# Empty places of the experts skipped by a bound on the index in the row gathers and scatters, with four fixed buffers for gathered rows

## The chip, the cores and the metric

The kernel runs on one core of one Trainium2 chip. The metric is device time in microseconds (us); lower is better. A core has five engines with instruction queues of their own, each worked off in order: PE (TensorE, matrix products), DVE (VectorE), ACT (ScalarE), POOL (GpSimd) and SP (SyncE, which here only starts transfers). Transfers run on 16 DMA engines that all queues share. "Landing" of a transfer is the moment its completion reaches the waiting engine.

## The reference, cut to what matters

A first block (two layers of a mixer) and a second block (linear attention, retention) come before the part that changes: a mixture of experts over 1024 tokens, with 32 experts, two for each token.

```python
def hier_moe(h, w_rg, b_rg, w_re, b_re, w_gate, w_up, w_down):
    ...
    expert_id = g_sel[:, None] * EXPERTS_PER_GROUP + top_i.astype(jnp.int32)
    ...
    def expert_block(args):
        xb, e = args
        hid = jax.nn.silu(xb @ w_gate[e]) * (xb @ w_up[e])
        return hid @ w_down[e]

    y = lax.map(expert_block, (x_pad.reshape(NB, MOE_BLOCK, D), block_e)).reshape(P, D)
    out = jnp.zeros((T, D), jnp.float32).at[tok_pad].add(y.astype(jnp.float32) * w_pad[:, None])
```

Each token of 1024 numbers goes to two experts, so 2048 pairs of token and expert are worked on. How many fall to each expert depends on the inputs. With the inputs of this case the counts, from the largest, are 173, 149, 149, 148, 145, 137, 136, 124, 98, 89, 70, 64, 62, 57, 57, 55, 49, 44, 44, 43, 28, 23, 20, 19, 18, 17, 10, 6, 6, 5, 3 and 0.

## The kernel before

The experts are the last large stage, after the output projection of the second block (`po`, which adds into `x`). The router (`router`, `choose`, `ranks`, `places`) finds for each token its two experts and its rank there, sorts the experts by their counts, and makes two index tables: `idh` (which token stands at a place, for reading) and `idy` (which row of the result, for writing). Each expert in the sorted order has a fixed number of places, whatever its count: ten have 192 (two blocks, of 128 and 64), four 128, four 96, eight 64 and six 48 (`CAPS`); that is 42 blocks with 3616 places for 2048 pairs. A place beyond an expert's count is empty; `index` adds 2048 + p to its index, so that it points behind the real rows:

```python
    hrow = dr.tile([1024 + 64, 2 * D], F16, name="hrow")
    yrow = dr.tile([2048 + 128, D], F32, name="yrow")
    ...
        vs(inv, cnt, pcol[:, j:j + 1], ALU.is_le, pcol[:, NJ:NJ + 1], MUL)
```

The work of an expert: `gather` reads the rows of its tokens (4 KB each) from `hrow` in DRAM into a tile `xg` by an indirect transfer from POOL's queue; `columns` transposes them on PE (`pxT`) and copies them on ACT (`xT`); `fetch_e` loads three weight matrices of 1 MB each through SP into `land`, splits each into a high half (`whi`, ACT) and a low half (`wlo`, DVE); `expert` multiplies (`pgu`), forms the hidden values (`mth`, `hid`), multiplies again (`pyd`), scales the result on DVE into `ysb`, and writes the rows of each block (4 KB each) to `yrow` by an indirect transfer from POOL's queue, the scatter. Empty places are read from rows of zeros behind the tokens (filled once, from `zr`) and written to rows behind the results.

The order: `turn` walks the experts, a large one and a small one in turns for most of the stage; rows are gathered two experts ahead, weights loaded two ahead; the second product of an expert and its scatter come after the first product of the next. The framework adds the waits. Three matter here: `xg` has four buffers, so a gather waits for the transposes of the one four before; `ysb` has two, so DVE waits for the landing of the scatter two blocks before; and all scatters write one tensor, so POOL starts a scatter only when the one before has landed.

Of the kernel before, what the change touches and what calls it, by code (L numbers as in the profile page):

```python
# [19 lines left out]
P = 128  # L20
# [33 lines left out]
def build(tc, a):  # L54
# [16 lines left out]
    def phase_pools(sizes):  # L71
        """the pools of a phase, in place of those of the phase before"""
# [7 lines left out]
    def psum_pools(sizes, level=0):  # L80
        """the eight banks, by use"""
# [20 lines left out]
    def slot(shape, dt=F32, name="sl"):  # L102
        """a 2 KB slot; views over it"""
        n = int(np.prod(shape[1:]))
        t = pools["t2"].tile([P, 516 if dt == F32 else 1032], dt, tag="t2", name=name)
        return view(t[:, :n], shape)
# [37 lines left out]
    # constants  # L144
# [16 lines left out]
    def rsqrt(out, ss, scale, eps, shape_n):  # L161
        """out = (ss * scale + eps) ** -0.5"""
# [15 lines left out]
    def units(src, n, k=KT):  # L178
        """weights [P, k x n] as [(k0, k1, hi, lo)], halves [P, k1 - k0, n]"""
# [12 lines left out]
    # ---- conditioning vectors  # L192
    def silu_cols(tag):
        """x * sigmoid(x) of two vectors, [128, 8, 2]"""
# [9 lines left out]
    def ada_groups(dst, wsrc, groups, cols):  # L204
        """dst[:, 4 g + j, v] = w[:, 512 g + 128 j + :]^T cols[v] of groups (g, vectors)"""
# [19 lines left out]
    # ---- norm of a block of tokens, feature-major, into hi/lo halves  # L225
    BLK = [(0, 256), (256, 512), (768, 512)]

    def add_square(acc, x, n, scale=1.0, place=None, eng=None):
        """acc + (scale x)^2"""
# [9 lines left out]
    def sum_rows(acc, n):  # L239
        """[128 tokens, n / 128]: the sums over the partitions of acc [128, n]"""  # L240
# [8 lines left out]
    def spread(rs, n, rb=None):  # L249
        """psum [128, n]: rs [128 tokens, n / 128] on every partition"""  # L250
# [29 lines left out]
    # ---- block 1  # L280
# [33 lines left out]
    def ada_ab(mod, bad, gn, c_sh, c_sc, v, tag):  # L314
        """h = y * A + B of a norm: A = SH g (1 + sc), B = SH sh"""
# [24 lines left out]
    def layer(l, hT, C, fetched, side, lead=iter(())):  # L340
# [25 lines left out]
        def qk_norm(ps, nh, i, g):  # L366
            """rope(rmsnorm(ps) * g), per head of 64; the second part writes it"""
# [75 lines left out]
        def queries(i):  # L443
            """the halves of q, feature-major, per head"""
# [8 lines left out]
        def maxima(i):  # L453
            """the maxima of the scores per head; they go with the high halves of q, beside ones under the low halves of k"""
# [27 lines left out]
        def weights(i, kv, k0, beside):  # L482
            """exp of the scores of two tiles of keys, [keys, heads x tokens], in halves"""
# [47 lines left out]
        def attention(tiles):  # L531
            """two tiles of keys at a time, for four heads: their weights, and the values of those two before; beside them the maxima of the next tile of tokens"""
# [29 lines left out]
        def half(H, i, name):  # L562
            """a 1 KB place for tile i, two to a slot"""
# [52 lines left out]
        def gelu2(ps):  # L616
            """2 gelu(x) of x = ps * F_IN"""
# [99 lines left out]
        def mlstm_state(d, t, nxt):  # L717
            """the state after tile t, which is what tile nxt starts from"""
# [86 lines left out]
        def aside(n=1):  # L805
            """a part of the work that later stages need"""
# [1429 lines left out]
```

## Time and profile before

| what | value |
|---|---|
| median of 3 runs | 3553.04 us (3533.69, 3553.04, 3561.47) |
| profiled execution: span from first to last instruction | 3555.6 us |
| profiled execution: own time | not marked among the three; the span lies 2.6 us above the median |
| PE busy over the span | 3151.0 us (89%) |
| DVE, ACT, POOL busy | 2282.1 (64%), 1494.3 (42%), 1058.6 us (30%) |
| bytes moved by DMA | 333.47 MB |
| first gather of the experts starts | at 3061.38 us |
| last scatter starts | at 3500.99 us |

The shares are averages over stages that differ. Until about 2950 us PE is the busiest engine; in the experts' stage it is at about three quarters, and the DMA engines are at 73 to 87%. The three runs lie 28 us apart, so a change below about 1% can hardly be told from none.

### The profile page before, as it was taken

To read this page: it belongs to the slowest core of one execution; us is meant where nothing else is said; L and a number is where in the kernel's file an instruction comes from. 1 tells how busy PE (TensorE), PEld (TensorE's weight loads), DVE (VectorE), ACT (ScalarE), POOL (GpSimd) and SP (SyncE) were. 2 spreads that over 40 slices of the span, in tenths; PEclk is the share of its full clock that TensorE was granted. 3 is DMA by queue.
4 is the path that set the end of the run, shared out by engine and by line. 5 is a ranking of instruction groups with operands and counts; after the bars stand their busy time and mean duration, and the time that the engine had idled before them with its cause. 6 is when DMAs were issued, how large, how long until landed. Compare 5 with 4: busy or idle time off the path is not lost. (4 is left out here: it accounts for less than half of the span.)

```text
span 3555.6 us, 59029 instructions
## 1 busy us (share of the span) xinstructions
PE 3151.0 (89%) x23404; PEld 1950.9 (55%) x23404; DVE 2282.1 (64%) x4559; ACT 1494.3 (42%) x2474; POOL 1058.6 (30%) x1208
## 2 busy tenths in 40 slices
PE   5999888899999889898999999999989999778772
PEld 1558455555548455644465655656644447556551
DVE  5878898843688899846374755747622223677565
ACT  3322366642323367633535335353312112466452
POOL 4211454432311555534031321313300002243432
PEclk8999899999999899999999999999999999798886
DMA  6320101103331111323101111011141121688775
GB/s 222 100 87 19 45 22 43 37 16 102 93 95 51 51 37 52 90 78 110 44 13 48 50 40 47 13 48 50 36 137 59 54 93 68 204 320 311 275 271 219
DMA packets 118559, 333.47 MB, mean 94 GB/s; under 512 B 14448, under 2 KB 35104, under 8 KB 109312
## 3 DMA queue, kind: packets, MB, share of 16 engines
q1 hardware_dynamic: 109184, 298.89, 25.8%
q0 software_dynamic: 9088, 30.71, 2.6%
q8 instruction: 186, 3.05, 0.4%
q14 instruction: 101, 0.83, 0.1%
HBM read 289.31 MB, written 40.24 MB: 93 GB/s over the span
## 5 line engine op out<-in xcount | busy, mean ns | idle before, releaser
L175 DVE SCALAR_TENSOR_TENSOR wlo<-land,whi 128x1024 f16<-128x1024 f32 (+3 forms) x289 | 419.0, 1467 | 187.1 <-ACT whi L140 185.1
L140 ACT ACTIVATE whi<-land 128x1024 f16<-128x1024 f32 (+3 forms) x289 | 352.6, 1230 | 301.9 <-DMA land<-wexp 82.5
L355 PE MATMUL pin<-whi,hhi 128*128 128x512 f16 (+2 forms) x1184 | 412.5, 348 | 22.8 <-DVE vlo L137 9.9
L356 PE MATMUL pin<-wlo,hhi 128*128 128x512 f16 (+2 forms) x1184 | 412.5, 348 | 1.3 <-DVE wlo L175 1.3
L357 PE MATMUL pin<-whi,hlo 128*128 128x512 f16 (+2 forms) x1184 | 411.3, 347 | 2.1 <-DVE hlo L121 2.0
L124 POOL TENSOR_TENSOR ptl<-pe,pth 128x512 f16<-128x512 f32 x164 | 214.1, 1308 | 184.9 <-ACT pth L140 98.6
L236 POOL TENSOR_TENSOR acc<-acc,sq 128x512 f32<-128x512 f32 (+1 forms) x74 | 80.4, 1094 | 566.3 <-ACT sq L140 563.2
L1171 PE MATMUL pvg<-whi,hhi 128*128 128x512 f16 (+1 forms) x640 | 229.5, 359 | 7.2 <-ACT gz L140 7.2
L1172 PE MATMUL pvg<-wlo,hhi 128*128 128x512 f16 (+1 forms) x640 | 229.7, 359 | 0.0
L1173 PE MATMUL pvg<-whi,hlo 128*128 128x512 f16 (+1 forms) x640 | 229.6, 359 | 0.0
L465 DVE TENSOR_REDUCE mx<-pmx 128x1 f32<-128x512 f32 (+1 forms) x400 | 219.7, 584 | 13.2 <-PE pmx L464 12.2
L140 ACT ACTIVATE pe<-S 128x512 f32<-128x512 f32 x328 | 181.4, 592 | 70.0 <-PE S L491 41.5
L137 DVE SCALAR_TENSOR_TENSOR acc<-wada,ccol,acc 128x512 f32<-128x512 f32 x224 | 174.3, 792 | 19.0 <-DMA wada<-ada 18.1
L464 PE MATMUL pmx<-kst,qst 128*128 128x512 f16 (+1 forms) x400 | 137.7, 357 | 46.0 <-DVE mx L465 25.8
L2032 POOL DMA_INDIRECT yrow<-ysb,idy x42 | 111.9, 2664 | 221.4 <-DMA yrow<-ysb,idy 93.2
L355 PEld LDWEIGHTS <-hhi 128*128 128x128 f16 x1184 | 119.4, 101 | 105.0 <-issue 12.5
L140 ACT ACTIVATE pth<-pe 128x1024 f16<-128x1024 f32 x164 | 173.2, 1056 | 5.2 <-PE pv L521 1.4
L357 PEld LDWEIGHTS <-hlo 128*128 128x128 f16 x1184 | 118.7, 100 | 101.0 <-issue 15.0
L356 PEld LDWEIGHTS <-hhi 128*128 128x128 f16 x1184 | 118.6, 100 | 96.7 <-issue 19.2
L2006 PE MATMUL pgu<-xT,whi 128*128 128x192 f16 (+4 forms) x1024 | 161.8, 216 | 0.0
L2005 PE MATMUL pgu<-xT,whi 128*128 128x192 f16 (+4 forms) x1024 | 161.7, 216 | 0.0
L520 PE MATMUL pv<-vhi,ptl 128*128 128x65 f16 x1312 | 150.6, 196 | 12.3 <-POOL ptl L124 11.6
(493 smaller groups left out, 8473.9 us busy)
## 6 DMA issues: line engine op xcount, KB each, us to landing
land<-wexp SPq DMA_DIRECT2D x62, 1024.0 KB
wada<-ada SPq DMA_DIRECT2D x160, 256.0 KB
land<-wexp SPq DMA_DIRECT2D x68, 512.0 KB
land<-win SPq DMA_DIRECT2D x48, 512.0 KB
land<-wout SPq DMA_DIRECT2D x24, 512.0 KB
land<-wgla SPq DMA_DIRECT2D x24, 512.0 KB
land<-wret SPq DMA_DIRECT2D x24, 512.0 KB
wada<-ada SPq DMA_DIRECT2D x16, 512.0 KB
```

The source lines that it names most:

```text
L124: return nc.gpsimd.tensor_tensor(out, i0, i1, op=op)
L137: return nc.vector.scalar_tensor_tensor(out, i0, s, i1, op0=op0, op1=op1, **kw)
L140: return nc.scalar.activation(out, in_, f, **kw)
L175: eng.scalar_tensor_tensor(lo[:, :n], land[:, :n], scale, hi[:, :n], op0=MUL, op1=SUB)
L355: nc.tensor.matmul(ps[:, :n], hh, whi[:, kt - k0], start=kt == 0, stop=False)
L356: nc.tensor.matmul(ps[:, :n], hh, wlo[:, kt - k0], start=False, stop=False)
L357: nc.tensor.matmul(ps[:, :n], hl, whi[:, kt - k0], start=False, stop=kt == KT - 1)
L465: nc.vector.tensor_reduce(mx[:, h, j:j + 1], ps[:, c], axis=AX.X, op=MAX)
L1171: nc.tensor.matmul(ps[:, :c1 - c0], hh, whi[:, kt - k0, c0:c1], start=kt == 0, stop=False)
L1172: nc.tensor.matmul(ps[:, :c1 - c0], hh, wlo[:, kt - k0, c0:c1], start=False, stop=False)
L1173: nc.tensor.matmul(ps[:, :c1 - c0], hl, whi[:, kt - k0, c0:c1], start=False, stop=kt == KT - 1)
L2006: nc.tensor.matmul(o, whi[:, kt - k0, c], xT[:, 1, kt, :N], start=False, stop=False)
```

## The change

Every indirect transfer of the experts gets a bound on its index, 1023 for reading and 2047 for writing, with places beyond it passed over instead of reported as an error. The rows behind the real ones in `hrow` and `yrow` go, and so do the tile `zr` and the transfer that filled them with zeros. A gathered tile now keeps what it held at the empty places, so `xg` becomes four tiles that are made once, set to zero once on POOL, and used in turn. The rest of the difference between the two files is comments.

```diff
-    hrow = dr.tile([1024 + 64, 2 * D], F16, name="hrow")
-    yrow = dr.tile([2048 + 128, D], F32, name="yrow")
+    hrow = dr.tile([1024, 2 * D], F16, name="hrow")
+    yrow = dr.tile([2048, D], F32, name="yrow")
...
-    zr = work([P, 1024], F16, name="zr")
-    nc.vector.memset(zr, 0.0)
-    nc.sync.dma_start(out=hrow[1024:1088, :].rearrange("p (a d) -> p a d", a=2), in_=zr[:64, None, :].to_broadcast([64, 2, 1024]))
...
-    mg = gstack.enter_context(tc.tile_pool(name="mg", bufs=4, side="right", reuse_waits="tile"))
+    mg = gstack.enter_context(tc.tile_pool(name="mg", bufs=1, side="right", reuse_waits="tile"))
...
+    rows_in = [mg.tile([P, 2 * D], F16, tag=f"xg{q}", name="xg") for q in range(4)]
+    for xg in rows_in:
+        nc.gpsimd.memset(xg, 0.0)
 
     def gather(e, j, n):
-        xg = mg.tile([P, 2 * D], F16, tag="xg", name="xg")
-        nc.gpsimd.indirect_dma_start(out=xg[:n], out_offset=None, in_=hrow[:, :],
+
+        xg = rows_in.pop(0)
+        rows_in.append(xg)
+        nc.gpsimd.indirect_dma_start(out=xg[:n], out_offset=None, in_=hrow[:, :], bounds_check=1023, oob_is_err=False,
                                      in_offset=bass.IndirectOffsetOnAxis(ap=idh[:n, j, e:e + 1], axis=0))
         return xg
...
-            nc.gpsimd.indirect_dma_start(out=yrow[:, :], out_offset=bass.IndirectOffsetOnAxis(ap=idy[:n, j, e:e + 1], axis=0),
+            nc.gpsimd.indirect_dma_start(out=yrow[:, :], bounds_check=2047, oob_is_err=False, out_offset=bass.IndirectOffsetOnAxis(ap=idy[:n, j, e:e + 1], axis=0),
                                          in_=ysb[:n], in_offset=None)
```

On POOL, between the last sums of squares of the output projection (`acc`) and the last scaled rows of the router (`hm`), the queue held these rows before:

```order
L236 TENSOR_TENSOR acc<-acc,sq 128x256 x5
L134 TENSOR_SCALAR rs_31013<-rst 128x2
L124 TENSOR_TENSOR rs_31013<-rs_31013,mhalf 128x2
L134 TENSOR_SCALAR hm<-hm,AB 128x256 x4
L124 TENSOR_TENSOR row<-hrf,row 128x512 x4
```

The same place of the changed kernel (`rs` is the root that scales a token's row, `row` the halves that go to `hrow`):

```order
L236 TENSOR_TENSOR acc<-acc,sq 128x256 x5
L1921 MEMSET xg 128x2048 x2
L134 TENSOR_SCALAR rs_31010<-rst 128x2
L1921 MEMSET xg 128x2048
L124 TENSOR_TENSOR rs_31010<-rs_31010,mhalf 128x2
L1921 MEMSET xg 128x2048
L134 TENSOR_SCALAR hm<-hm,AB 128x256 x4
L124 TENSOR_TENSOR row<-hrf,row 128x512 x4
```

Four settings to zero have come in, two of them between the steps that make `rs` and `hm`. In the middle of the experts' stage POOL's queue held these gathers and scatters before, with the semaphores that each waits for (DMASW: the landing of an earlier transfer of this queue):

```order
L2032 DMA yrow<-ysb,idy 2176x1024 [waits DMASW1_49,DMASW0_49,DVE_49]
L1925 DMA xg<-hrow,idh 64x2048 [waits PE_49]
L2032 DMA yrow<-ysb,idy 2176x1024 [waits DMASW1_49,DVE_49]
L1925 DMA xg<-hrow,idh 48x2048 [waits DMASW4_49,PE_49]
L1925 DMA xg<-hrow,idh 128x2048 [waits DMASW6_49,PE_49]
L2032 DMA yrow<-ysb,idy 2176x1024 [waits DMASW3_49,DVE_49]
```

and in the changed kernel:

```order
L2034 DMA yrow<-ysb,idy 2048x1024 [waits DMASW1_49,DMASW0_49,DVE_49]
L1927 DMA xg<-hrow,idh 64x2048 [waits PE_49]
L2034 DMA yrow<-ysb,idy 2048x1024 [waits DMASW1_49,DVE_49]
L1927 DMA xg<-hrow,idh 48x2048 [waits DMASW4_49,PE_49]
L1927 DMA xg<-hrow,idh 128x2048 [waits DMASW6_49,PE_49]
L2034 DMA yrow<-ysb,idy 2048x1024 [waits DMASW3_49,DVE_49]
```

Nothing has moved here: the order and the waits are the same, and the tensor that is written has 128 rows fewer. Not shown in these rows, POOL's queue also has a write of the bound into a register ahead of each indirect transfer.

## Rows read from the trace of the kernel before

**Rows 1.** the page: busy us by engine, share of span, instructions

```profile
PE 3151.0 (89%) x23404; PEld 1950.9 (55%) x23404; DVE 2282.1 (64%) x4559; ACT 1494.3 (42%) x2474; POOL 1058.6 (30%) x1208
```

**Rows 2.** the page: DMA queues (q1 SP, q0 POOL): packets, MB, engine share

```profile
q1 hardware_dynamic: 109184, 298.89, 25.8%
q0 software_dynamic: 9088, 30.71, 2.6%
```

**Rows 3.** experts' stage: busy us PE, PEld, DVE, ACT, POOL; clock; DMA share; GB/s

```profile
3100.00:3500.00 400.00, 307.74 (x3914) 223.38 (x3913) 269.89 (x286) 225.48 (x244) 153.93 (x73) 0.89 0.82 284
```

**Rows 4.** who waited for whom, 3100 to 3500 us: total us, times, longest

```profile
POOL yrow L2032 <- DMA yrow<-ysb,idy: 93.2, 16, 9.2
DVE ysb L121 <- DMA yrow<-ysb,idy: 75.9, 17, 8.8
ACT whi L140 <- DMA land<-wexp: 70.6, 55, 3.6
POOL yrow L2032 <- issue: 56.2, 10, 9.1
```

**Rows 5.** POOL in time order, mid-stage: start, us, operation, idle before

```profile
3327.58 8.31 POOL L2032 DMA_INDIRECT yrow<-ysb,idy  x1 [3.32 <-DVE ysb L121]
3343.89 4.56 POOL L2032 DMA_INDIRECT yrow<-ysb,idy  x1 [8.00 <-issue]
3348.75 0.98 POOL L1925 DMA_INDIRECT xg<-hrow,idh  x1 [0.30 <-issue]
3353.86 2.97 POOL L2032 DMA_INDIRECT yrow<-ysb,idy  x1 [4.14 <-DMA yrow<-ysb,idy]
...
3362.90 8.30 POOL L2032 DMA_INDIRECT yrow<-ysb,idy  x1 [3.54 <-DVE ysb L121]
```

**Rows 6.** DVE in order of time, same stretch

```profile
3326.91 0.68 DVE L121 TENSOR_TENSOR ysb<-pyd,g2r 64x512 f32<-64x512 f32 x1 [1.96 <-DMA yrow<-ysb,idy]
...
3334.95 0.54 DVE L137 SCALAR_TENSOR_TENSOR mth<-mth,pgu 128x384 f32<-128x384 f32 x1
3343.25 0.68 DVE L121 TENSOR_TENSOR ysb<-pyd,g2r 48x512 f32<-48x512 f32 x1 [7.76 <-DMA yrow<-ysb,idy]
```

**Rows 7.** POOL in order of time, the last scatters (blocks of 128, then 96)

```profile
3442.14 3.03 POOL L2032 DMA_INDIRECT yrow<-ysb,idy  x1 [5.19 <-issue]
3453.95 0.96 POOL L2032 DMA_INDIRECT yrow<-ysb,idy  x1 [8.78 <-DMA yrow<-ysb,idy]
3463.10 1.89 POOL L2032 DMA_INDIRECT yrow<-ysb,idy  x1 [8.18 <-DMA yrow<-ysb,idy]
3474.14 0.92 POOL L2032 DMA_INDIRECT yrow<-ysb,idy  x1 [9.15 <-issue]
...
3491.90 0.91 POOL L2032 DMA_INDIRECT yrow<-ysb,idy  x1 [3.50 <-issue]
```

**Rows 8.** gathers: ns min/median/max, first and last start

```profile
L1925 POOL DMA_INDIRECT xg<-hrow,idh x42: 889/943/4935, 3061.4 to 3436.1; - x42
```

**Rows 9.** scatters, same columns

```profile
L2032 POOL DMA_INDIRECT yrow<-ysb,idy x42: 877/1726/8707, 3101.5 to 3501.0; - x42
```

**Rows 10.** scatters on the page: count, busy us, mean ns; idle before, releaser

```profile
L2032 POOL DMA_INDIRECT yrow<-ysb,idy x42 | 111.9, 2664 | 221.4 <-DMA yrow<-ysb,idy 93.2
```

**Rows 11.** POOL's settings to zero of comparable size: count, busy us, mean ns

```profile
L398 POOL MEMSET klz<- 64x2560 f16 x2 | 4.5, 2226 | 0.1
```

**Rows 12.** POOL in order of time at the router's last rows

```profile
3028.85 0.76 POOL L236 TENSOR_TENSOR acc<-acc,sq 128x256 f32<-128x256 f32 x1 [1.26 <-ACT sq L140]
3037.57 0.19 POOL L134 TENSOR_SCALAR rs<-rst 128x2 f32<-128x2 f32 x1 [7.96 <-DVE rst L246]
3037.84 0.72 POOL L124 TENSOR_TENSOR rs<-rs,mhalf 128x2 f32<-128x2 f32 x1
3039.86 0.55 POOL L134 TENSOR_SCALAR hm<-hm,AB 128x256 f32<-128x256 f32 x1 [1.30 <-DVE hm L121]
```

**Rows 13.** the transfer from the zero tile: ns and start

```profile
L1693 SPq DMA_DIRECT2D hrow<-zr x1: 611/611/611, 2921.3 to 2921.3; - x1
```

## The prediction

> **What bounds the kernel now.** The page's busy times come first [rows 1]: PE leads over the whole span, but the change touches only the experts' stage, from about 3061 to 3510 us. In 400 us of that stage [rows 3] PE is busy 308, DVE 270 and the DMA engines 82%: no engine is full, so the stage is held by waits. The list of waits [rows 4] says which. POOL stands before a scatter for the landing of the scatter before, 93.2 us in 16 waits, and another 56.2 us in 10 waits marked "issue" are the same thing: in time order each of those shown follows a scatter and lasts 8 to 9 us [rows 5, 7]. DVE waits 75.9 us, 17 times, for a scatter to land before it may overwrite `ysb`; while it does, it makes no low halves of weights and frees no `land` buffer. ACT's 70.6 us for weights are spread over 55 short waits.
>
> So the stage is a chain: a scatter is issued, lands, and only then the next starts. 42 scatters between 3101.5 and 3501.0 us [rows 9] are 41 steps of 9.74 us. One stretch shows it [rows 5, 6]. DVE gets its buffer at 3326.91 and works without a gap until 3335.49; the scatter of 3327.58 is not done issuing until 3335.89, 0.4 us later, so its 8.31 us are DVE's run; then both stand until that scatter lands (8.00 us on POOL, 7.76 us on DVE). A step has three parts: DVE's run, the issue (at least 0.88 us), the landing. The change touches the third.
>
> **The rows that go.** 3616 places hold 2048 pairs, so 1568 rows of 4 KB are no longer written and 1568 no longer read. The gap from the end of a scatter to the start of the next prices a row. After blocks of 128 places it is 8.00 [rows 5], 8.78, 8.18 and 9.15 us [rows 7], mean 8.53 (8.78 is 3453.95 less 3442.14 + 3.03, the others likewise). After a block of 64 it is 3353.86 - 3348.45 = 5.41, after one of 48 it is 3362.90 - 3356.83 = 6.07 [rows 5], mean 5.74 at 56 places. That is 2.79 us over 72 places, 0.039 us a row: the upper end. The lower end is what a row takes alone: POOL's queue used 2.6% of 16 engines' span for 9088 packets [rows 2], 0.026 x 3555.6 x 16 / 9088 = 0.163 us, and over 16 engines 0.010 us. I take the middle, 0.024, since weights share the engines but not all the time. Then 1568 rows are 38 us of landing (16 to 61). Not all of it is on the path: of 221.4 us that POOL idles before scatters [rows 10] 149 are landings by name, two thirds, and some of the rest are waits for DVE that itself waited for a landing; I count three quarters. **Minus 28 us (12 to 46).** What is late next is DVE's own work, 270 of 400 us, then PE's 308; both leave room for this much.
>
> Seven of the ten large experts have a full first block, and their scatters keep their length; the gain falls to the second blocks (three of them now empty), the small experts and the tail, where blocks of 128 hold 57 to 70 rows.
>
> **What the gathers and the engines get.** The gathers are not waited for by PE in the list, but stand ahead of some scatters in the same queue. The 3136 rows together free 3136 x 0.163 / 16 = 32 us of the DMA engines' time, at 82% use. ACT's 70.6 us for weights could shrink by a like share, but weights start late because `land` comes free late, not because bytes are slow. **Minus 5 us (0 to 16)**, near the low end, for the scatters behind a gather.
>
> **What is added.** Four settings of 128x2048 to zero on POOL. The nearest row is 2226 ns for 2560 elements a partition [rows 11], so 2048 take 1.78 us. Where they stand matters [rows 12]. The first waits for PE's last reads of the buffers that lay there; POOL is free from 3029.61 to 3037.57, and two (3.56 us) fit in. The third stands between the two steps of `rs`, and everything from the router's products to the first gather is behind it: 1.78 us. The fourth stands before `hm`, which came 1.30 us after `rs` was done, so 0.48 us shows. **Plus 2.3 us** (0 if they run at once, 7.1 if none is hidden).
>
> Each of the 84 indirect transfers now has a register write ahead of it on POOL. It stands ahead of the wait, so it runs while POOL would wait anyway: nothing; without that cover it would be less than the 0.30 us that POOL shows between two transfers already [rows 5], and for 42 scatters under 13 us.
>
> The zero tile's transfer took 611 ns of SP's queue at 2921 us [rows 13], when PE was multiplying without a break and later loads were already queued: nothing, at most 0.6 us. The four fixed tiles are used in the same turn as the four buffers, and the waits in the queue are the same: nothing.
>
> The issues stay. They were 111.9 us for 42 scatters [rows 10] against a shortest of 0.88 [rows 9]; the excess is DVE's runs, not rows [rows 5, 6]. If it were the writing of descriptors, 43% of 75 us would go as well, 32 us. The Trainium skill, "SBUF — State Buffer", section "Who interferes with whom", says that a DVE instruction with two SBUF inputs keeps out a GpSimd instruction that reads SBUF until it is done; by that rule the excess does not depend on the rows, and the trace agrees, with the 0.4 us after DVE's end.
>
> **The sum** is -28 - 5 + 2.3 = -31. Against the profiled execution's own span, 3555.6 - 31 = 3524.6. The span lies 2.6 us above the median of the three runs, and what lies around it is not listed; from the median it would be 3522. I put 3524.
>
> **Rivals.**
>
> *The stage follows the bytes.* Against it: no DMA queue is full over the stage. For it: 82% is high, landings of 8 us where an undisturbed 96-place block takes 3.50 us [rows 7] are made by neighbours, and fewer bytes shorten every landing, also those of full blocks. 12.8 of 284 x 0.4 = 113.6 MB go [rows 3], 11.3%; of 400 us that is 45, and with descriptors no longer written for skipped rows somewhat more. 3555.6 - 45 - 5 + 2.3 = 3508.
>
> *A landing is mostly fixed.* Skipped places are the last of each block. If a block's rows are dealt to the 16 engines in runs, the engines with the first rows have as much as before and the landing stays, but for empty blocks. For it: even 96 places cost 3.50 us when nothing else runs, of which 96 x 0.010 is 1 us. The gain is then the low end, 12 us, less 2.3: 3546. The Trainium skill, "DMA: Bandwidth & Descriptors", section "Anatomy of one DMA — SWDGE (gpsimd) path", gives such a transfer about 2 us fixed plus its bytes at 436 GB/s; by that a row is 0.0094 us, and 1568 rows at three quarters 11 us, this rival's result. The trace of the loaded stage, at 0.039, disagrees; its undisturbed tail does not.
>
> *The bound does not skip.* The packets stay, and only the zeroing shows: 3558.
>
> *Slower: the test of the index.* POOL now compares each index, and builds descriptors for some places only. The issue of a gather takes 0.89 us at least and 0.94 at the median [rows 8]; no row shows one with a bound. Each us more on a scatter is a us on the chain, 42 in all, and a longer issue meets more of DVE's runs. It cancels the gain at 31 / 42 = 0.74 us a scatter, and makes the kernel slower by over 1% at (31 + 36) / 42 = 1.6 us. At 2 us: 3555.6 + 84 - 31 = 3609. Against it: 48 and 128 places issue in nearly the same time when DVE is still, so work per place is small.
>
> **How the numbers follow.** About 1%, 36 us, is what a measurement here can tell from no change. The forecast has 0.44, with its own range 3509 to 3541 (slopes of 0.039 and 0.014); 0.08 of it lies beyond 1%. The bytes have 0.28 (faster by over 1%), the fixed landing and the bound without effect 0.16 together (within 1%), the slower issue 0.12, of which 0.02 within 1%. So faster 0.36, within 1% 0.54, slower 0.10. The range goes from 3492, which cuts off the strongest part of the bytes' case, to 3560, which takes in both cases without gain and leaves out the slower issue.
>
> **What would show it.** Packets of POOL's queue fall from 9088 by 3136 to 5952, or the bound does nothing. The step between scatters falls from 9.74 to about 9.0 us, with the gap after small and empty blocks shorter and that after full ones as before; if full ones shorten too, the bytes' case is right. The shortest issue stays at 0.88 us, or the test costs. DVE's wait for `ysb` falls well below 75.9 us. The first gather starts about 2 us later relative to the last `acc` of the router. The prediction is wrong if landings fall and the steps do not, with another wait in their place on POOL or DVE.

## The result and the profile after

The changed kernel takes 3499.61 us (median of 4 runs, 3496.67 to 3511.56), beside 3551.47 us for the kernel before (median of 4 runs, 3533.69 to 3561.47). The medians lie 52 us apart. The ratio is 0.9881, with a 95% interval of 0.9844 to 0.9918: by it 42 us less, 29 to 55 by the interval. (Ratios, here and below, are those on record, from fast runs alone; they are not quotients of the medians, and the two can differ by some us.) The time lies in the stated range of 3492 to 3560, 24 us below the predicted 3524, but outside the 3509 to 3541 that the sum itself allowed; and the larger chance, 0.54, was on a change within 1%. The profiled execution took 3496.67 us, of which its span is 3494.8.

The first view is the page of the changed kernel: busy times, the packets of all queues, and POOL's own queue (`q0`).

```profile
PE 3140.3 (90%) x23404; PEld 1947.2 (56%) x23404; DVE 2279.9 (65%) x4558; ACT 1492.3 (43%) x2474; POOL 1018.9 (29%) x1212
...
DMA packets 118416, 320.38 MB, mean 92 GB/s; under 512 B 17569, under 2 KB 38225, under 8 KB 109169
...
q0 software_dynamic: 9088, 17.88, 1.5%
```

Against [rows 1, 2], PE, DVE and ACT work as before. POOL's queue moves 17.88 MB in place of 30.71: the bound works. But its packets are 9088 still. A place that is passed over leaves a packet: on the page of the kernel before 14448 packets were under 512 bytes, now 17569, which is 3121 more for 3136 places. (In POOL's queue alone the trace has it exactly: packets of 4 bytes rose from 1520 to 4656, packets of 4096 bytes fell from 7456 to 4320, 3136 each.)

Next the experts' stage, which now ends before 3445 us: first the busy times from 3100 to 3440 us (PE, PEld, DVE, ACT, POOL; granted clock; DMA share; GB/s), then the waits from 3100 to 3445 us (total us, times, longest one).

```profile
3100.00:3440.00 340.00, 297.34 (x3914) 218.47 (x3913) 270.91 (x288) 223.74 (x244) 105.85 (x73) 0.94 0.86 303
```

```profile
POOL yrow L2034 <- DMA yrow<-ysb,idy: 70.4, 14, 9.0
ACT whi L140 <- DMA land<-wexp: 55.1, 38, 4.2
POOL yrow L2034 <- DVE wlo L175: 42.5, 6, 8.9
...
POOL yrow L2034 <- DVE ysb L121: 33.0, 8, 7.0
...
POOL yrow L2034 <- issue: 16.3, 5, 6.4
...
DVE ysb L121 <- DMA yrow<-ysb,idy: 5.1, 4, 2.4
```

PE is now busy 297 of 340 us (87%), where [rows 3] had 308 of 400 (77%); DVE 80% for 67%, DMA 0.86 for 0.82. The same 3914 matmuls take 297.34 us for 307.74, at a granted clock of 0.94 in the mean for 0.89: some 10 us of PE's time came with a higher clock while PE stood less, and no run separates the two. The waits of [rows 4] have not all shrunk alike. DVE's, before it refills `ysb`, went from 75.9 us in 17 waits to 5.1 us in 4: it is all but gone. POOL's for a landing went by the list from 93.2 to 70.4 us, but here the names mislead. The trace also holds the landing of each scatter (the last update of the semaphore that its completion raises), and all six waits put down to DVE's `wlo` (42.5 us), of which a scatter needs nothing, end 0.75 to 0.78 us after the landing of the scatter before. Counted so, 36 of 41 scatters started on a landing before the change, and 30 of 41 still do.

The scatters and the gathers by themselves (ns least, median, most; first and last start), then the scatters with their busy and mean time and the idle time before them:

```profile
L2034 POOL DMA_INDIRECT yrow<-ysb,idy x42: 877/1021/3475, 3102.8 to 3442.2; - x42
```

```profile
L1927 POOL DMA_INDIRECT xg<-hrow,idh x42: 934/995/4967, 3064.1 to 3381.3; - x42
```

```profile
L2034 POOL DMA_INDIRECT yrow<-ysb,idy x42 | 65.0, 1549 | 191.7 <-DMA yrow<-ysb,idy 70.4 <-DVE wlo L175 42.5 <-DVE ysb L121 33.0
```

41 steps from 3102.8 to 3442.2 us are 8.28 us each, where [rows 9] give 9.74: 60 us, as much as the two spans differ. The shortest scatter is 877 ns as before and the shortest gather 934 for 889 [rows 8]. But the sum of the scatters' issues fell from 111.9 us [rows 10] to 65.0, the longest from 8707 ns to 3475. With the landings from the trace the 41 steps can be split (sums in us; in a few cases some updates of the semaphore are missing from the trace, so the split is good to some us):

| | issue | from its end to the landing | from there to the next start | all |
|---|---|---|---|---|
| before | 111.0 | 245.9 | 42.6 | 399.5 |
| changed | 64.2 | 221.8 | 53.4 | 339.4 |

Of the 60 us, 47 are shorter issues. The landings give 24, of which 11 are lost again in later starts.

One stretch with the same blocks as [rows 5, 6], a large expert's second block of 64 and a small one's of 48; first DVE, then POOL:

```profile
3328.09 0.68 DVE L121 TENSOR_TENSOR ysb<-pyd,g2r 64x512 f32<-64x512 f32 x1 [1.03 <-PE pyd L2032]
3330.03 6.76 DVE L175 SCALAR_TENSOR_TENSOR wlo<-land,whi 128x2048 f16<-128x2048 f32 x4 [1.26 <-ACT whi L140]
3336.71 0.55 DVE L137 SCALAR_TENSOR_TENSOR mth<-mth,pgu 128x384 f32<-128x384 f32 x1
3337.17 0.68 DVE L121 TENSOR_TENSOR ysb<-pyd,g2r 48x512 f32<-48x512 f32 x1
...
3343.06 2.29 DVE L175 SCALAR_TENSOR_TENSOR wlo<-land,whi 128x2048 f16<-128x2048 f32 x1 [0.74 <-ACT whi L140]
```

```profile
3326.41 1.01 POOL L2034 DMA_INDIRECT yrow<-ysb,idy  x1 [1.30 <-DVE mth L121]
3335.09 1.37 POOL L2034 DMA_INDIRECT yrow<-ysb,idy  x1 [7.66 <-DVE wlo L175]
...
3343.19 2.95 POOL L2034 DMA_INDIRECT yrow<-ysb,idy  x1 [4.86 <-DMA yrow<-ysb,idy]
```

In [rows 6] DVE stands 7.76 us after `mth` until a scatter has landed. Here the same refill, at 3337.17, follows `mth` at once: its buffer is free. And the scatter of 3335.09 begins late in a DVE run and takes 1.37 us, where that of 3327.58 in [rows 5] began 0.67 us after a refill that the same landing had released, at the start of DVE's run, and took 8.31. So it is throughout the trace of the kernel before: all ten issues of more than 3.1 us (3.79 to 8.71 us) begin 0.64 to 0.68 us after such a refill. The 17 issues that begin so are together 56 us over 0.9 us each, the other 25 only 18; in the changed kernel 4 begin so, with 2.5 us, and the other 38 have 25. One thing did not shrink: the scatter of 3335.09 is one of the three blocks that now hold no row at all, and from its end to the next start it is 3343.19 - 3336.46 = 6.73 us, where it was 5.41.

The settings to zero, in order of time on POOL:

```profile
3030.26 0.77 POOL L236 TENSOR_TENSOR acc<-acc,sq 128x256 f32<-128x256 f32 x1 [1.26 <-ACT sq L140]
3030.96 3.54 POOL L1921 MEMSET xg<- 128x2048 f16 x2
...
3038.28 1.80 POOL L1921 MEMSET xg<- 128x2048 f16 x1
...
3040.73 1.80 POOL L1921 MEMSET xg<- 128x2048 f16 x1
...
3064.09 1.17 POOL L1927 DMA_INDIRECT xg<-hrow,idh  x1 [5.11 <-DVE over L121]
```

They stand where the prediction put them (two in the idle stretch, the third and fourth around the second step of `rs`), 1.80 us each. From the start of the last `acc` to the first gather it is 33.83 us, before 3061.38 - 3028.85 = 32.53 [rows 8, 12]: 1.3 us more.

### The profile page after: what moved, and what is told of

The parts are those of the page before. It is cut to its first block, busy times and chain, and to the rows that moved or that the text cites. A ratio compares the mean times of both kernels' runs of the same rounds, so it can differ in the third digit from the quotient of the medians.

```text
span 3494.8 us, 59113 instructions
## 1 busy us (share of the span) xinstructions
PE 3140.3 (90%) x23404; PEld 1947.2 (56%) x23404; DVE 2279.9 (65%) x4558; ACT 1492.3 (43%) x2474; POOL 1018.9 (29%) x1212
## 2 busy tenths in 40 slices
DMA packets 118416, 320.38 MB, mean 92 GB/s; under 512 B 17569, under 2 KB 38225, under 8 KB 109169
## 3 DMA queue, kind: packets, MB, share of 16 engines
q0 software_dynamic: 9088, 17.88, 1.5%
## 5 line engine op out<-in xcount | busy, mean ns | idle before, releaser
L2009 PE MATMUL pgu<-xT,wlo 128*128 128x192 f16 (+4 forms) x1024 | 161.2, 215 | 0.0
```

## Experiments

Three theories were set against each other. **A, the tie**: before the change DVE's refill of one of the two `ysb` buffers waits for a landing, and the next scatter's issue, which the same landing releases, waits behind the DVE run that now begins, so that runs, issues and landings stand in a row; somewhat shorter landings let them slip past each other. **B, the bytes**: 12.8 MB fewer are moved, and everything waits less for DMA. **C, landing by rows**: the prediction's sum, a price per row on the chain of landings. They were set up after the result was known, and before each run.

The kernel before was timed anew beside each group: 3555.74 us (25 runs) for the first four, 3535.04 (12 runs) for the next four, 3550.53 (11 runs) for the last four. Its single runs lay 51 to 58 us apart in each group (3526.39 to 3576.92 in the first); ratios go against the group's own.

### One half of the change at a time

```
-    yrow = dr.tile([2048 + 128, D], F32, name="yrow")
+    yrow = dr.tile([2048, D], F32, name="yrow")
...
-    nc.gpsimd.indirect_dma_start(out=yrow[:, :], out_offset=...
+    nc.gpsimd.indirect_dma_start(out=yrow[:, :], bounds_check=2047, oob_is_err=False, out_offset=...
```

> The kernel before with the bound on the scatters alone; gathers still read rows of zeros into four turning buffers, and nothing is set to zero on POOL. Three theories stand. A, the tie: DVE waits for a scatter to land before it may refill one of two result buffers, and the scatter's issue waits behind DVE's run; landings that are a little shorter let the two slip past each other, so nearly the whole gain comes from scatters: about 3505 us, DVE's wait for the result buffer under 20 us, the 42 issues together near 65 us. B, the bytes: half of the skipped rows go, so half of the gain: about 3525 us. C, the landing by rows (the prediction's sum): the gain is scatters' rows, 25 to 30 us: about 3522 us, with the issues still near 110 us.

Measured: 3520.0 us (10 runs), ratio 0.9897 (0.9865 to 0.993).

The other half is the changed kernel with these two lines as before, so that the gathers alone have the bound and the fixed buffers.

> The changed kernel with its scatters as before (no bound, 128 spare rows behind the results). A, the tie: landings of scatters stay, so the tie stays: 3540 to 3555 us, DVE's wait for the result buffer 60 us or more. B, the bytes: half of the gain, about 3525 us, DMA share of the stage lower by some 4 points. C, the landing by rows: about 5 us less than before from scatters that stand behind a gather, 3547 us.

Measured: 3537.05 us (10 runs), ratio 0.9947 (0.9902 to 0.9991). Each half leaves out 6.4 MB, and POOL's queue moved 24.30 MB in both. By the medians the scatters gained 36 us and the gathers 19, together about what the whole gained (52). What fell is the same in both: DVE's wait for a landing from 75.9 us to 52.3 and 53.1, and the issues from 111.9 us to 96.5 and 96.1. No theory foresaw both. For the scatters A's 3505 us, with the wait under 20 us and the issues near 65, missed; B's 3525 and C's 3522 came near. For the gathers A's wait of 60 us or more missed, and B's 3525 and C's 3547 lie on either side. The interval of the gathers' half, 3 to 35 us, holds the 5 us that C gave it. The pair decides nothing alone; that shorter gathers, which write no `yrow`, go with a shorter wait of DVE for a scatter is all that it shows.

### A third result buffer instead of the bound

The control makes room, without any bound; the experiment uses that room for a third `ysb`.

```
-    ... (("mp", 5), ("mx", 2), ("mw", 3), ("my", 2)))
-    pools["w2"] = mpool("w2m", 2)
+    ... (("mp", 5), ("mx", 2), ("mw", 2), ("my", 2)))     (control; the experiment: ("my", 3))
+    pools["w2"] = mpool("w2m", 1)
```

> The control for the next run: the kernel before with hidden values in two buffers in place of three and one spare work tile in place of two, which frees the room that a third result buffer needs. All theories: as before within 1%, 3535 to 3570 us; if it is slower than that, the hidden values needed their third buffer and the next run is read against this one.

> The control with a third result buffer, no bound anywhere: same bytes, same rows, same order of instructions; DVE now waits for the scatter three blocks before. A, the tie: the gain comes without any skipped row, 35 to 55 us below the control; DVE's wait for the result buffer falls below 20 us and the 42 issues from about 110 to about 70 us. B and C: bytes and rows are the same, so no more than 10 us below the control, with the wait moved to POOL.

Measured: control 3540.68 us (10 runs), ratio 0.9956 (0.9916 to 0.9995); three buffers 3512.86 us (4 runs, only 4 us apart), ratio 0.989 (0.9853 to 0.9927). No byte, row or packet is left out, and the gain over the kernel before is nearly that of the change (0.989 for 0.9881). Below the control it is 28 us, less than A's 35 to 55, though all four runs lie below the control's fastest. In the profile of the run with three buffers the waits, the scatters and the stage read:

```profile
POOL yrow L2032 <- DMA yrow<-ysb,idy: 107.4, 20, 9.3
ACT whi L140 <- DMA land<-wexp: 74.1, 62, 3.3
```

```profile
L2032 POOL DMA_INDIRECT yrow<-ysb,idy x42: 880/1109/4180, 3110.7 to 3457.1; - x42
```

```profile
3100.00:3440.00 340.00, 291.56 (x3780) 213.79 (x3779) 269.17 (x277) 229.14 (x247) 99.07 (x71) 0.92 0.96 337
```

DVE's wait for a landing does not appear any more. The issues are down to 60.6 us in all, their longest to 4180 ns, though every scatter carries all its places. So the issues shrink when DVE is untied from the landings: their length is not rows. The landings did not shrink (255.1 us from the issues' ends, 245.9 before), and POOL's wait for them did not go: 107.4 us in 20 waits by the list, and 40 of 41 scatters start on a landing. The chain of scatter, landing and scatter still stands, and each step has lost the long issue. This is A against B and C. B may have a share all the same: the DMA engines are now at 0.96 with 337 GB/s, nearly full. The control is a caution: two pools made smaller gave 15 us by themselves (by the ratio 2 to 30), with issues of 73.1 us in its profile, which is of one of its faster runs (3523.33). That the tied stage depends on how runs and landings happen to meet would explain it, and fits the times (53 us between runs of the control, 3519.91 to 3572.80, and 4 with three buffers).

### Both, and the scatters by turns into two tensors

Bound and three buffers together are the changed kernel with the pool sizes of the experiment above.

> The changed kernel with three result buffers in place of two (and two of the pool of hid, one of the half tiles, as in the run with three buffers without the bound; 3512.9 there, 3499.6 with the bound alone). Theory A (the tie between DVE's refill and the landings was nearly all of the gain; either cure takes it): what is left for the second cure is small, 3490 to 3505, with DVE's wait for a landing at 0 and the scatters' issues at 55 to 65 us. Theory B (the bytes left out are the gain): the buffers free the queue and 12.8 MB less are moved beside it, so the two gains add up, 3455 to 3475. Theory C (landing by rows, the chain of landings is the bound): the buffers change nothing of the chain, 3495 to 3505, the steps of the scatters stay at 8.3 us.

Measured: 3498.1 us (4 runs), ratio 0.99 (0.9859 to 0.9941), steps of (3444.35 - 3107.63) / 41 = 8.21 us, issues 59.9 us. That is the time of the changed kernel: the two gains do not add up, which speaks against B (3455 to 3475) as the main part. C expected the same time, for another reason.

The next pair goes at the prediction's chain itself. A control reads the last part's rows from the weights, and so leaves the experts' results out of the output; in the experiment, which leaves them out too, the scatters alternate between two tensors, so POOL no longer waits for the landing right before.

```
-   nc.sync.dma_start(out=y, in_=yrow[2 * P * i:2 * P * (i + 1), :]...          (control and experiment)
+   nc.sync.dma_start(out=y, in_=a["wexp"][i][:, :2 * D].rearrange("p (k d) -> p k d", k=2))
...
+    yrow2 = dr.tile([2048 + 128, D], F32, name="yrow2")                       (experiment)
+    yturn = [yrow, yrow2]
...
+            yturn.append(yturn.pop(0))
-            nc.gpsimd.indirect_dma_start(out=yrow[:, :], out_offset=...
+            nc.gpsimd.indirect_dma_start(out=yturn[0][:, :], out_offset=...
```

> Control for the next run: the kernel before, but the last part reads rows of the weights in place of the experts' results, so the sum of the experts' rows is left out of the output; the scatters are done as before. All theories: the expert stage as in the kernel before (41 steps of 9.4 to 9.8 us), only the last loads no longer wait for the last landing, 0 to 10 us less, 3530 to 3560.

> The control, with the scatters going by turns into two tensors, so that none waits for the landing of the one right before it; rows, bytes, buffers and order of instructions stay (the sum of the experts' rows is left out here too). The prediction's view of the stage (a chain of scatter, landing, scatter): the chain is cut, the step falls from about 9.5 us to what is late next, 8.2 to 8.8 us, 30 to 55 us off the control. Theory A (DVE's refill of one of two buffers waits for a landing, and the issue behind DVE's run): the refill still waits for the landing two scatters back, but that comes earlier as POOL no longer waits, 15 to 35 us off, issues still above 80 us. Theory B (bytes at the rate that the DMA engines give): within 10 us of the control.

Measured: control 3554.44 us (7 runs), ratio 1.0045 (0.9994 to 1.0096), steps of 9.60 us; two tensors 3504.94 us (6 runs), ratio 0.9907 (0.9859 to 0.9954), steps of (3458.58 - 3113.00) / 41 = 8.43 us. 50 us off the control (30 off this group's runs of the kernel before; every run lies below every run of the control), again with all rows and bytes. The waits and the stage with two tensors:

```profile
POOL yrow L2035 <- DVE ysb L121: 107.2, 29, 9.7
...
DVE ysb L121 <- DMA yrow<-ysb,idy: 3.4, 1, 3.4
```

```profile
3100.00:3440.00 340.00, 290.58 (x3741) 213.04 (x3738) 264.87 (x273) 225.25 (x242) 94.66 (x71) 0.92 0.95 337
```

The prediction's view of the stage, a chain of scatter, landing and scatter, is borne out: cut it, and the stage is 8.4 us a step. A had the size too small (15 to 35 us) and the issues wrong (over 80 us; they are 57.6). POOL's wait for the landing and DVE's hang together, but not both ways: cutting POOL's took DVE's with it (70.5 us in the control, 3.4 with two tensors), while the third buffer took DVE's and left POOL's. What either takes away is the long issue.

### A scatter by itself

Nothing of the kernel but its scatter, repeated. `idx` has 128 places of which 128, 64, 20 or 0 are valid.

```
    def scatters(k, n, times):
        for _ in range(times):
            nc.gpsimd.indirect_dma_start(out=yrow[:, :], bounds_check=2047, oob_is_err=False,
                out_offset=bass.IndirectOffsetOnAxis(ap=idx[:n, k:k + 1], axis=0), in_=ysb[:n], in_offset=None)
    CASES = ((0, 128), (1, 128), (2, 128), (3, 128), (0, 64))
    for k, n in CASES:
        scatters(k, n, 6)
    ...
    for j in range(96):
        nc.sync.dma_start(out=lands[j % 3], in_=w[j // 3][:, (j % 3) * 2048:(j % 3 + 1) * 2048])
    ...
    for k, n in CASES:
        scatters(k, n, 6)
    ...
    for j in range(40):
        nc.vector.scalar_tensor_tensor(lo, big, 2.0, hi, op0=ALU.mult, op1=ALU.subtract)
    scatters(0, 128, 8)
    scatters(3, 128, 8)
```

> Not the kernel but its scatter by itself, nothing else of the reference is computed: scatters of 128 places with 128, 64, 20 and 0 of them valid and of 64 places all valid, six of each one after the other into one tensor; then the same beside a stream of 1 MB weight loads on SP's queue; then 8 full and 8 empty ones beside DVE runs of 128x2048 with two operands of SBUF. The prediction's sum had 0.024 us for each row passed over (0.010 to 0.039): by it (theory C) a step of 128 rows is 3.1 us (1.3 to 5.0) longer than one of none, alone as well as beside the loads, and one of 64 lies in the middle. Theory A needs no price per row, and expects a landing that is mostly fixed: empty against full 0.3 to 1.5 us alone, both 1 to 4 us longer beside the loads. Issue 0.9 to 1.0 us in all cases without DVE; beside the DVE runs (2 us each) it is several us by both theories, and if that is the issue's whole length it is as long for an empty scatter as for a full one.

It ran once, with a span of 455.5 us. In order of time on POOL, the first scatter of each case, alone (to 97.50) and then beside the loads; a `MEMSET` waits for the last landing before it:

```profile
3.39 1.11 POOL L36 DMA_INDIRECT yrow<-ysb,idx  x1 [1.72 <-DMA idx<-idx]
...
25.02 0.96 POOL L36 DMA_INDIRECT yrow<-ysb,idx  x1 [2.61 <-DMA yrow<-ysb,idx]
...
45.75 0.96 POOL L36 DMA_INDIRECT yrow<-ysb,idx  x1 [2.51 <-DMA yrow<-ysb,idx]
...
62.74 0.96 POOL L36 DMA_INDIRECT yrow<-ysb,idx  x1 [1.87 <-DMA yrow<-ysb,idx]
...
76.75 0.91 POOL L36 DMA_INDIRECT yrow<-ysb,idx  x1 [1.38 <-DMA yrow<-ysb,idx]
...
97.50 0.95 POOL L46 MEMSET ysb<- 128x1024 f32 x1 [2.36 <-DMA yrow<-ysb,idx]
...
106.95 1.04 POOL L36 DMA_INDIRECT yrow<-ysb,idx  x1 [0.17 <-issue]
...
160.97 0.96 POOL L36 DMA_INDIRECT yrow<-ysb,idx  x1 [7.66 <-DMA yrow<-ysb,idx]
...
213.35 0.96 POOL L36 DMA_INDIRECT yrow<-ysb,idx  x1 [7.98 <-DMA yrow<-ysb,idx]
...
261.32 0.96 POOL L36 DMA_INDIRECT yrow<-ysb,idx  x1 [7.22 <-DMA yrow<-ysb,idx]
...
307.97 0.91 POOL L36 DMA_INDIRECT yrow<-ysb,idx  x1 [7.23 <-DMA yrow<-ysb,idx]
...
349.53 0.95 POOL L55 MEMSET ysb<- 128x1024 f32 x1 [5.88 <-DMA yrow<-ysb,idx]
```

A sixth of the distance between two such rows is a step:

| places, valid | alone, us a step | beside loads, us a step |
|---|---|---|
| 128, 128 | 3.61 | 9.00 |
| 128, 64 | 3.46 | 8.73 |
| 128, 20 | 2.83 | 8.00 |
| 128, 0 | 2.34 | 7.78 |
| 64, 64 | 3.46 | 6.93 |

Three readings. From 128 valid places to none it is 1.27 us alone and 1.23 beside the loads, 0.0098 us a row in the mean, the prediction's lower end and well below the 0.024 that it took. (It is no straight line: alone, 128 to 64 valid places is 0.0023 us a row, 64 to none 0.0175.) An empty scatter of 128 places still takes 7.78 us beside the loads; a landing is mostly fixed there, and what the loads add, 5.4 us to a full one as to an empty one, is more than A's 1 to 4. And 64 places, all valid, are 1.8 us shorter than 128 places of which 64 are valid, beside the loads but not alone: by this one pair, what is paid beside loads is the place, valid or not, 0.028 us for one passed over. Issues are 0.9 to 1.1 us in every row. The loads are a heavier neighbour than the kernel's: the DMA engines are at 1.00 with 402 to 421 GB/s here, at 0.82 with 284 GB/s in [rows 3].

Beside DVE (a row of DVE, then four of POOL: two full scatters, the first empty one and a later empty one):

```profile
361.58 69.76 DVE L60 SCALAR_TENSOR_TENSOR lo<-big,hi 128x2048 f16<-128x2048 f32 x30 [361.58 <-POOL hi L58]
...
383.60 2.04 POOL L36 DMA_INDIRECT yrow<-ysb,idx  x1 [2.61 <-DMA yrow<-ysb,idx]
388.26 2.04 POOL L36 DMA_INDIRECT yrow<-ysb,idx  x1 [2.62 <-DMA yrow<-ysb,idx]
...
406.91 2.00 POOL L36 DMA_INDIRECT yrow<-ysb,idx  x1 [2.65 <-DMA yrow<-ysb,idx]
...
412.62 0.96 POOL L36 DMA_INDIRECT yrow<-ysb,idx  x1 [1.36 <-DMA yrow<-ysb,idx]
```

30 DVE instructions in 69.76 us are 2.325 us each. The issue of 383.60 starts 1.09 us into the tenth, and ends at 385.64, 0.8 us after that one's end at 384.83. The first empty one, of 406.91, starts 1.16 us into the 20th, and ends 0.83 us after it: 2.00 us. The later empty ones, such as that of 412.62, start 0.1 us before an instruction's end and take 0.96 us, as alone. So an issue that falls into one of these DVE instructions (both inputs in SBUF) is held to its end, full or empty, and its length goes by where it falls. Here the rule of the Trainium skill that the prediction named ("SBUF — State Buffer", "Who interferes with whom") shows without anything else beside it. What it does not show is an issue of several DVE instructions, which both A and C had expected here. In the kernel before, the issue of 3327.58 to 3335.89 [rows 5] spans these, and the `mth` of [rows 6]:

```profile
3327.68 2.28 DVE L175 SCALAR_TENSOR_TENSOR wlo<-land,whi 128x2048 f16<-128x2048 f32 x1
3329.88 0.68 DVE L121 TENSOR_TENSOR ysb<-pyd,g2r 64x512 f32<-64x512 f32 x1
3330.48 4.54 DVE L175 SCALAR_TENSOR_TENSOR wlo<-land,whi 128x2048 f16<-128x2048 f32 x3
```

Those are six instructions in a row; here it is never more than the rest of one. When an issue gets in between two DVE instructions and when not stays open.

### The four on one chip

The last group sets bound and buffers against each other beside the same runs of the kernel before: the kernel with three buffers and the one with both once more, the changed kernel itself, and the changed kernel with two tensors (which leaves the experts' results out of the output, as above):

```
+    yrow2 = dr.tile([2048, D], F32, name="yrow2")
+    yturn = [yrow, yrow2]
...
+            yt = yturn.pop(0)
+            yturn.append(yt)
-            nc.gpsimd.indirect_dma_start(out=yrow[:, :], bounds_check=2047, ...
+            nc.gpsimd.indirect_dma_start(out=yt[:, :], bounds_check=2047, ...
...
-        nc.sync.dma_start(out=y, in_=yrow[2 * P * i:2 * P * (i + 1), :]...
+        nc.sync.dma_start(out=y, in_=a["wexp"][i][:, :2 * D].rearrange("p (k d) -> p k d", k=2))
```

> The kernel before with three result buffers (the same kernel as in the run of that name), now beside the next three, so that the bound's worth can be read where DVE's refill never waits. All theories: 3505 to 3518.

> Bound and three buffers again, beside the run before. Theory A (what the bound gave was mostly the freed loop of refill, issue and landing; the rest is the price of the rows as measured by the scatter by itself, 1.2 us for 128, so about 15 us for 1568): 10 to 20 us below the run with three buffers alone, 3490 to 3505. Theory B (12.8 MB at the 337 GB/s that the three buffers reached): 30 to 40 us below, 3470 to 3485. If a row costs nothing once the loop is free: within 5 us.

> The changed kernel with its scatters going by turns into two tensors and the last part reading weights in place of results (the sum of the experts' rows is left out), so no scatter waits for the landing right before it. If the chain scatter, landing, scatter still bounds the stage after the change (POOL's waits for a landing are 70 us there, the step 8.28 us): the step falls to 7.4 to 7.9 us, 3465 to 3485. If after the change the stage is held by the engines and the bytes, and POOL's wait has slack: within 8 us of the changed kernel, less a few us at the end for the last loads that no longer wait, 3488 to 3502.

> The changed kernel itself, beside the three runs before. Theory A: as with bound and three buffers, within 6 us, 3495 to 3508. If two buffers still hold it back: 10 us or more above that run.

| us (median; 6 runs, 11 of the kernel before) | two buffers | three buffers |
|---|---|---|
| no bound | 3550.53 | 3513.10 (3505.36 to 3519.22) |
| bound | 3501.74 (3493.11 to 3521.35) | 3495.32 (3486.85 to 3504.25) |

Where the third buffer has opened the loop, the bound is worth 17.8 us (all six runs of the one lie above all six of the other): within A's 10 to 20, close to 1568 rows x 0.0098 us = 15, and half of B's 30 to 40. With two buffers it is worth 48.8. So about 31 us of the change's gain go with the opened loop and 18 with rows and bytes; with such spreads each is good to some 10 us. (The right column has the smaller pools of the control too, which may hold some of the difference; the bound was not run with these and two buffers.) That the 18 are the price of the rows is not shown: in these two traces the landings fall from 259.1 to 216.7 us, and 17 us of it are lost in later starts (40.7 to 57.7). The third buffer on top of the bound gives 6.4 us, between the two outcomes that were named, and there the runs overlap. With the bound alone the tie is not quite gone: this group's trace of the changed kernel has an issue of 8.28 us, which began 0.68 us after a refill that had waited for the same landing. Ratios to the kernel before: 0.989 (0.9855 to 0.9925), 0.9874 (0.9833 to 0.9915) for the changed kernel, 0.9838 (0.9803 to 0.9874) for both, the best complete version here.

The changed kernel with two tensors took 3493.0 us (6 runs), 8.7 us below the changed kernel, some of it from last loads that wait for nothing. Its waits and stage:

```profile
POOL yrow L2038 <- DVE ysb L121: 92.6, 28, 9.6
```

```profile
3100.00:3440.00 340.00, 298.10 (x3999) 221.27 (x3997) 276.56 (x288) 231.72 (x253) 96.11 (x72) 0.95 0.87 310
```

POOL and DVE wait for a landing once each, 1.8 and 1.9 us, and the steps are (3446.47 - 3113.12) / 41 = 8.13 us against 8.28, outside the 7.4 to 7.9 of a chain that still bounds. Cutting the chain took 50 us before the change and takes at most 9 after it: most steps still begin on a landing, but what would hold them next is nearly as late. PE at 88%, DVE at 81% and the DMA engines at 0.87 are within two hundredths of the row of the changed kernel. That these, together, hold the stage now is argued from the shares; no run took one of them away.

## Why the prediction was right, and where not

**The stage is a chain that waits.** Right, and shown by cutting it (3554.44 to 3504.94 us). What the prediction missed is that the long issues hang on DVE's wait and vanish with it.

**"The issues stay."** This is the step that failed: it put at nothing the largest term of all, 47 of the 60 us by which the stage fell. Its reason was right: the excess is DVE's runs, not rows. Its conclusion was not: 111.9 us became 65.0, and 60.6 without any bound, since the long issues are those that begin together with DVE's refill on the same landing, and a refill that need not wait for the landing no longer starts a DVE run there.

**The price of a row**, "I take the middle, 0.024". As the price of a row it is too high by more than two. The slope of 0.039 us came from blocks of different size, 128 places against 56. The scatter by itself shows nearly the same slope beside loads, (9.00 - 6.93) / 64 = 0.032, but it belongs to the place: passing a place over saves only the 0.0098 of its row. The amount came out all the same: from the issue's end to the landing, the sum is 246 to 259 us in the six traces without any bound and 212 to 222 in the five with both, about 35 us less, where 38 was foreseen. That is luck in part. The bound on the gathers alone took 16 us of it (229.7), from scatters that still write every place, and the three blocks left without a row kept their landing (5.97 us in the mean of the six traces, 5.84 in that of the five). Lighter traffic beside the scatters, the argument of *The stage follows the bytes*, would explain the first and not the second; what shortens the landings stays open. The share on the path was too high: three quarters, where 11 of 24 us came back as later starts, though 36 of 41 starts had hung on a landing. So the -28 was 13 in the trace of the result.

Two errors of opposite sign, about 15 us too much for the landings and 47 of issues left out, are most of the difference between the 31 us foreseen and the 61 us by which the two profiled spans differ. That the time lies in the stated range is luck in part: the sum's own range ended at 3509, and the lower end of 3492 was set for the bytes' case.

**The gathers**, -5 (0 to 16): the run with the gathers' half gave -19, with an interval from 3 to 35 that holds the 5. Its trace has a gain that the term did not foresee: DVE's wait and the scatters' issues were shorter (53.1 and 96.1 us).

**What is added.** Settings to zero +2.3, measured 1.3, in the places foreseen. The register writes take no time that shows, the shortest gather 45 ns more. Zero tile and fixed tiles: nothing that shows.

**The rivals.** *The bytes* came nearest in time (3508), and the bound with the loop open is worth 17.8 of its 45 us. *A landing is mostly fixed* described the landing rightly (7.78 of 9.00 us remain) and the time wrongly, 3546, since the loop was not in it. The formula of the Trainium skill that it named ("DMA: Bandwidth & Descriptors", "Anatomy of one DMA — SWDGE (gpsimd) path") is met alone in its slope from 128 valid places to none, 0.0099 us a row for 0.0094, though not between 128 and 64 (0.0023); beside loads the fixed part is several us longer than it says. *The bound does not skip* fell with the 17.88 MB; its mark was badly chosen, since 9088 packets were to mean that it does nothing. *The test of the index* fell with the unchanged 877 ns of the shortest scatter; and a place passed over still gets its packet, so work is not left out there either.

**The signs.** Steps were to fall to about 9.0 us and fell to 8.28; DVE's wait fell as foreseen; the shortest issue stayed. The seven full blocks kept their landings (42.7 us together before, 41.5 after), as foreseen, but in the other traces their sum varies from 40 to 52 us; the empty second blocks did not shorten, against what was foreseen.

## What to carry to other kernels

Where two engines wait for the same landing and one of them also holds up the other's issue, price the loop and not its links: any cure that opens it (a third buffer, a second target tensor, or fewer rows) brought nearly the same time here, and two cures did not add up. Where a list of waits names an engine whose work the waiting one does not need, look in the trace for what ended just before. A price per row taken from blocks of different size is a price per place; measure it with places of which some are passed over. After a wait is removed, look again at every issue that was called fixed.

## What the hardware showed that was not expected

- A place passed over by the bound is not free: it leaves a packet (9088 before and after), and beside loads costs 0.028 us (one pair of cases) of the 0.032 that a written one does. A scatter of 128 places that writes nothing takes 2.34 us alone and 7.78 beside loads.
- Alone, 64 rows take nearly as long as 128 (3.46 and 3.61 us), while 20 and 0 are shorter (2.83 and 2.34).
- An issue on POOL that begins within a DVE instruction with both inputs in SBUF was held to its end when nothing else ran: 2.04 us for 0.96 with a full scatter, 2.00 with an empty one. In the kernel an issue that began with DVE's run was held for up to six instructions, 8.31 us.
- The times of the tied stage spread: 51 to 58 us between runs of the kernel before in each group, 4 and 14 in the two groups of the one with three buffers.
- A scatter that waits for nothing but the landing of the one before starts 0.74 to 0.82 us after it, in 36 of 41 steps before and 30 of 41 after.
